# The order of the SBUF pools in a two-layer hybrid trunk: weights low, activations in the middle

## The chip, the core and the metric

The kernel runs as one program on one core of one Trainium2 chip. The core has a matrix engine (TensorE, PE in the rows; its weight loads are rows of PEld), a vector engine (DVE), a scalar engine (ACT), a helper engine (POOL, GpSimd) and a queue engine (SP) that issues the transfers between HBM and the on-chip memory SBUF. SBUF has 128 partitions; a tile takes the same byte range in each of them, so that one byte address per tile says where it lies. Matrix results go to a second memory, PSUM. The metric is the device time of one execution in microseconds (us); the kernel before takes 2235.08 us, median of 3 runs (2234.99 to 2235.28).

## The reference

One sequence of 1024 tokens with 1024 channels goes through two layers. All weights and activations are float32.

```python
# layer 0: h = rms_norm(x);  x += lru_sb_mixer(h)
proj = h @ w_in                                     # 1024 -> 512 gate, 512 rec, 3 x 512 q,k,v
y_lru = gelu(gate) * rg_lru(conv4(x_rec), ...)      # linear recurrence over time
y_sb  = stick_breaking_attention(q, k, v)           # 8 heads of 64, blocks of 128 queries
x = x + concat(y_lru, y_sb) @ w_out
# layer 1: h = rms_norm(x);  x += conformer_conv_module(h)
u = h @ pw1_w + pw1_b
u = u[:, :1024] * sigmoid(u[:, 1024:])
u = causal_depthwise_conv(u, dw_w) + dw_b           # width 31
x = x + silu(layer_norm(u)) @ pw2_w + pw2_b
# after each layer: h = rms_norm(x);  a = relu(h @ w1);  x += (a * a) @ w2   (1024 -> 4096 -> 1024)
# at the end: rms_norm(x) * final_g
```

## The kernel before, in words

The sequence is worked on in two chunks of 512 tokens (a and b in the names of the rows, `_a` and `_b`). Every large product is made from three matmuls: each float32 operand is split into a high part and a low part in the type float32r (`wh`, `wl` for weights; `hh`, `hl`, `ah`, `al`, `y..h`, `y..l`, `s..h`, `s..l` for activations), and `mm3` (lines 153 to 160) adds low-high, high-low and high-high into one PSUM bank. Each of these matmuls has a stationary operand of 128x128, read by a weight load (PEld) of 128 columns, that is 512 bytes of each partition, and a moving operand of 128x512, that is 2048 bytes of each partition. There are two forms:

- `colmm` (lines 161 to 163): a weight slice is stationary and a normed activation moves. It makes `xg`, `q`, `k` (input projection), `pg`, `pv` (the Conformer's first projection, `pw1`), and `m` (first half of the MLP, `m1` inside `mlp`). Per output tile: 8 slices of the contraction, 3 matmuls each, 24 in all.
- `rows_into_x` (lines 235 to 240) and `v_cols`: an activation slice is stationary and a weight row moves. It makes `v`, `o_wo` (output projection), `o_q` (the Conformer's second projection, `pw2`), and `o_a`, `o_b` (second half of the MLP, `m2`). Per output tile of the last three: 4 slices, 12 matmuls.

In 512-column float32r matmuls that is 3072 of `m`, 3072 of `o_a` and `o_b`, 768 of `pg` and `pv`, 384 each of `xg`, `o_q` and `o_wo`, 192 each of `q`, `k` and `v`, and 96 of the attention's `z`.

Where the tiles lie is decided by pools. A pool takes a contiguous range of SBUF when it is opened, each range above the one before, in the order of the `tc.tile_pool` lines; inside a pool each tag has its slots (`bufs`) one after the other. The pools are:

- `cp` (line 43): constants, among them the identity of the transposes. A 64-byte tile `pad_cp` is part of it.
- `hp_` (line 44, 48 slots of 2048 bytes): the residual `x` and every split activation that is not the MLP's: `hh`, `hl`, `y..h`, `y..l`, `s..h`, `s..l`, also the attention's `ks` and `vt`. `ht`, `hf` and `xt_` (lines 52 to 59) take from it.
- `wp` (line 45): two raw weight buffers of 8192 bytes, which the transfers fill, and four each of `wh` and `wl` of 4096 bytes, which ACT and DVE write (`split_w`, `col_units`) and TensorE reads.
- `lp` (line 46, 8 slots): the convolution's inputs `u` and the recurrent branch's tiles, taken by `lt`.
- `sp` (line 47): small statistics; a 64-byte tile `pad_sp` (line 50) is its first.
- above them, by turns in the same range, `p1` (attention and recurrence: tags a, q, r and the gate weights `gaw`, `gxw`) and `p2` (tag b, 11 slots for the MLP's `r`, `ah`, `al`; tag c, 9 slots).

The order of the instructions on each engine comes from a scheduler that works from dependencies and modelled durations, together with hand-written pacing (`paced`, `waiting`, `tc.issue_after`, `tc.high_priority`).

Of the kernel before, what the change touches and what calls it, by code (L numbers as in the profile page):

```python
# [31 lines left out]
def tile_hybrid_trunk(  # L32
# [8 lines left out]
    V, A, T, Q = nc.vector, nc.scalar, nc.tensor, nc.gpsimd  # L41

    cp = ctx.enter_context(tc.tile_pool(name="cp", bufs=1))
    hp_ = ctx.enter_context(tc.tile_pool(name="hp", bufs=48))
    wp = ctx.enter_context(tc.tile_pool(name="wp", bufs=4))
    lp = ctx.enter_context(tc.tile_pool(name="lp", bufs=8))
    sp = ctx.enter_context(tc.tile_pool(name="sp", bufs=12))
    ps = ctx.enter_context(tc.tile_pool(name="ps", bufs=2, space=PSUM))

    sp.tile([P, 16], F32, tag="pad", bufs=1, name="pad_sp")  # L50
# [742 lines left out]
```

## Time and profile before

| What | Value |
|---|---|
| median of 3 runs | 2235.08 us |
| the profiled execution: its own time | 2235.9 us |
| its span, first to last instruction | 2234.1 us |
| TensorE busy | 2195.6 us (98%), 10180 matmuls |
| DVE, ACT, POOL busy | 1412.5, 954.3, 110.6 us (63%, 43%, 5%) |
| chain that ended last: PE, DVE, ACT | 95%, 3%, 1% |
| mean granted TensorE clock | 0.996 |

A matmul's row has its start and a recorded length. Matmuls overlap in the pipeline, so that the recorded length (389 ns in undisturbed stretches) is longer than the distance from one start to the next; this distance is what a stretch costs, and it is a stretch's length over its number of matmuls. The recorded length follows it: when the next start comes 6 ns later, it is some 6 ns longer.

### The profile page before, as it was taken

Reading aid. Unit: us, or ns where it says so; the run is one execution under the profiler, and the core shown is the slowest. Engines: PE = TensorE matmul, PEld = TensorE weight load, DVE = VectorE, ACT = ScalarE, POOL = GpSimd, SP = SyncE. Lnnn points to the kernel's source line nnn. Section 1 sums busy time; section 2 is a strip of 40 time slices with the busy share of each in tenths; the row PEclk is TensorE's granted clock in tenths of the full one; section 3 lists DMA queues with packets and bytes.
Section 4 is the critical chain, followed back from the end, with each engine's and each line's share of the span. In section 5 each row is a group of like instructions: output and inputs, shape, how many; then the busy total and the mean of one; then the engine's idle time right before and its main releaser. Section 6 shows DMA issues by size and latency. Waiting matters only on the chain.

```text
span 2234.1 us, 25970 instructions
## 1 busy us (share of the span) xinstructions
PE 2195.6 (98%) x10180; PEld 1770.6 (79%) x10180; DVE 1412.5 (63%) x1934; ACT 954.3 (43%) x1509; POOL 110.6 (5%) x296
## 2 busy tenths in 40 slices
PE   7999999999999999999999999999999999999998
PEld 5877776688888888888888888788888888888887
DVE  4387877855443444479898664999886555444344
ACT  4467677535333334333333363433333535333332
POOL 1000000000000001100000010300000001000000
PEclk9999999999999999999999999999999999999999
DMA  4111014012222223332223223233232234222222
GB/s 159 57 41 36 34 53 151 27 59 76 95 94 94 95 95 99 108 100 82 93 96 108 81 94 94 85 97 99 89 99 91 93 106 140 95 95 95 95 94 76
DMA packets 172010, 199.25 MB, mean 89 GB/s; under 512 B 5648, under 2 KB 120688, under 8 KB 171888
## 3 DMA queue, kind: packets, MB, share of 16 engines
q1 hardware_dynamic: 171872, 197.59, 27.2%
q8 instruction: 80, 1.31, 0.2%
q14 instruction: 42, 0.34, 0.0%
q10 hardware_dynamic: 16, 0.00, 0.0%
HBM read 190.23 MB, written 7.34 MB: 88 GB/s over the span
## 4 chain that ended last, share of the span: by engine, by line
PE 95%; DVE 3%; ACT 1%; issue 1%; DMA 0%; POOL 0%; SPq 0%; DVEq 0%; POOLq 0%; ACTq 0%
PE o_b L157 5%; PE o_a L157 5%; PE o_b L158 5%; PE o_a L159 5%; PE o_b L159 5%; PE o_a L158 5%; PE m_a L157 5%; PE m_a L159 5%; PE m_b L159 5%; PE m_b L157 5%; PE m_a L158 5%; PE m_b L158 5%; PE av L529 2%; PE wt L521 1%; PE xg L158 1%; PE xg L157 1%
## 5 line engine op out<-in xcount | busy, mean ns | idle before, releaser
L647 DVE SCALAR_TENSOR_TENSOR cv<-u,dwT,cv 128x512 f32<-128x512 f32 x480 | 340.0, 754 | 0.2
L157 PE MATMUL o_a<-wh_w2a,al_a 128*128 128x512 f32 x512 | 202.4, 396 | 0.0
L157 PE MATMUL o_b<-wh_w2b,al_b 128*128 128x512 f32 x512 | 202.3, 395 | 0.0
L158 PE MATMUL o_a<-wl_w2a,ah_a 128*128 128x512 f32 x512 | 202.2, 395 | 0.0
L159 PE MATMUL o_b<-wh_w2b,ah_b 128*128 128x512 f32 x512 | 202.1, 395 | 0.0
L158 PE MATMUL o_b<-wl_w2b,ah_b 128*128 128x512 f32 x512 | 202.1, 395 | 0.0
L159 PE MATMUL o_a<-wh_w2a,ah_a 128*128 128x512 f32 x512 | 201.6, 395 | 0.0
L125 ACT CAST wh_w1b<-raw_w1b 128x1024 fp32r<-128x1024 f32 x64 | 67.2, 1050 | 219.4 <-PE o_b L159 200.9
L125 ACT CAST wh_w1a<-raw_w1a 128x1024 fp32r<-128x1024 f32 x64 | 67.1, 1051 | 213.3 <-PE o_a L159 203.6
L105 DVE TENSOR_TENSOR wl_w2a<-raw_w2a,wh_w2a 128x1024 fp32r<-128x1024 f32 x64 | 78.3, 1223 | 124.1 <-ACT wh_w2a L104 124.1
L105 DVE TENSOR_TENSOR wl_w2b<-raw_w2b,wh_w2b 128x1024 fp32r<-128x1024 f32 x64 | 80.3, 1254 | 118.2 <-ACT wh_w2b L104 118.2
L240 DVE TENSOR_TENSOR xr<-o_a,xr 128x512 f32<-128x512 f32 x128 | 87.5, 686 | 81.0 <-PE o_a L159 80.1
L240 DVE TENSOR_TENSOR xr<-o_b,xr 128x512 f32<-128x512 f32 x128 | 87.9, 687 | 76.5 <-PE o_b L159 75.5
L159 PEld LDWEIGHTS o_b<-wh_w2b,ah_b 128*128 128x128 f32 x512 | 96.5, 188 | 22.5
L159 PEld LDWEIGHTS o_a<-wh_w2a,ah_a 128*128 128x128 f32 x512 | 96.5, 188 | 22.4
L158 PEld LDWEIGHTS o_b<-wl_w2b,ah_b 128*128 128x128 f32 x512 | 96.5, 188 | 22.3
L158 PEld LDWEIGHTS o_a<-wl_w2a,ah_a 128*128 128x128 f32 x512 | 96.5, 188 | 22.1
L157 PEld LDWEIGHTS o_a<-wh_w2a,al_a 128*128 128x128 f32 x512 | 96.4, 188 | 22.2
L157 PEld LDWEIGHTS o_b<-wh_w2b,al_b 128*128 128x128 f32 x512 | 96.4, 188 | 22.2
L252 ACT ACTIVATE r_b<-m_b 128x512 f32<-128x512 f32 x64 | 38.4, 600 | 169.3 <-PE m_b L159 169.3
L252 ACT ACTIVATE r_a<-m_a 128x512 f32<-128x512 f32 x64 | 38.4, 600 | 164.1 <-PE m_a L159 159.7
L126 DVE TENSOR_TENSOR wl_w1b<-raw_w1b,wh_w1b 128x1024 fp32r<-128x1024 f32 x64 | 77.9, 1220 | 37.9 <-ACT wh_w1b L125 37.9
(537 smaller groups left out, 5344.4 us busy)
## 6 DMA issues: line engine op xcount, KB each, us to landing
raw_w1a<-in_mlp_w_dram SPq DMA_DIRECT2D x32, 1024.0 KB, 5.1
raw_w2a<-in_mlp_w_dram SPq DMA_DIRECT2D x32, 1024.0 KB, 5.1
raw_w1b<-in_mlp_w_dram SPq DMA_DIRECT2D x32, 1024.0 KB, 5.2
raw_w2b<-in_mlp_w_dram SPq DMA_DIRECT2D x32, 1024.0 KB, 5.0
raw_pw<-in_od_pw_w_dram SPq DMA_DIRECT2D x32, 512.0 KB, 4.5
raw_q<-in_od_pw_w_dram SPq DMA_DIRECT2D x8, 1024.0 KB, 4.9
raw_wo<-in_ev_w_out_dram SPq DMA_DIRECT2D x6, 768.0 KB, 5.2
xa<-in_x_dram SPq DMA_DIRECT2D x16, 256.0 KB, 5.2
```

Source lines behind the costliest of these rows:

```text
L105: paced(V.tensor_tensor(lo, raw, hi.bitcast(F32), op=ALU.subtract), 1)
L125: A.copy(hi, srcs[i])
L126: paced(V.tensor_tensor(lo, srcs[i], hi.bitcast(F32), op=ALU.subtract), 2)
L157: T.matmul(acc, ll, rh, start=(i == 0), stop=False)
L158: T.matmul(acc, lh, rl, start=False, stop=False)
L159: T.matmul(acc, lh, rh, start=False, stop=(i == n - 1))
L240: paced(V.tensor_tensor(xt[t][h], acc, xt[t][h], op=ALU.add), 1.5)
L252: A.activation(r, acc, AF.Relu)
L521: T.transpose(pt[:, b * P:(b + 1) * P], ke[:, b * P:(b + 1) * P], ident)
L529: ins = T.matmul(av[j * 64:j * 64 + 64, tt * P:(tt + 1) * P], vt[lo_s // P + b][:, hc:hc + 64], wts[j][:, b * P:(b + 1) * P], start=(diag ...
L647: waiting.append(lambda k=k, m=m: V.scalar_tensor_tensor(cv[m], u[m][:, k:k + C], dwT[:, k * KT + m:k * KT + m + 1], cv[m], op0=ALU.mult, ...
```

## The change

The line that opens `hp_` moves from second to fifth place. Nothing else in the program is changed; the line numbers after it go up by one.

```diff
     cp = ctx.enter_context(tc.tile_pool(name="cp", bufs=1))
-    hp_ = ctx.enter_context(tc.tile_pool(name="hp", bufs=48))
+
     wp = ctx.enter_context(tc.tile_pool(name="wp", bufs=4))
     lp = ctx.enter_context(tc.tile_pool(name="lp", bufs=8))
     sp = ctx.enter_context(tc.tile_pool(name="sp", bufs=12))
+    hp_ = ctx.enter_context(tc.tile_pool(name="hp", bufs=48))
     ps = ctx.enter_context(tc.tile_pool(name="ps", bufs=2, space=PSUM))
```

The instructions of all five engines stand in the same order as before, with the same tiles in the same slots of their pools and the same semaphore waits. What differs is the byte address of every tile of four pools. In bytes of a partition:

| Pool | Before | After | First byte modulo 256, before and after |
|---|---|---|---|
| `wp`: raw, then `wh`, `wl` | 118528 to 167680 | 20224 to 69376 | 0 and 0 |
| `lp` | 167680 to 185088 | 69376 to 86784 | 0 and 0 |
| `sp` | 185088 to 187776 | 86784 to 89472 | 0 and 0 |
| `hp_` | 20224 to 118528 | 89472 to 187776 | 0 and 128 |
| `p1`, `p2` | from 187776 | from 187776 | 128 and 128 |

The slots of `hp_` (2048 bytes), of `wh` and `wl` (4096) and of `p2` (2048) are multiples of 256, and each stationary slice is 512 bytes, so that every such operand has its pool's remainder modulo 256. Exceptions above 187776 are the attention's `q` tiles in `p1` (212736 and up) and `gaw`, `gxw` (200448, 202496), all at remainder 0 because of the sizes of the slots below them; and the slots of `lp`, 2176 bytes apart, are at 0 and 128 by turns.

## Rows read from the trace of the kernel before

**Rows 1.** The page: engines with their busy time, then the chain by engine

```profile
PE 2195.6 (98%) x10180; PEld 1770.6 (79%) x10180; DVE 1412.5 (63%) x1934; ACT 954.3 (43%) x1509; POOL 110.6 (5%) x296
...
PE 95%; DVE 3%; ACT 1%; issue 1%; DMA 0%; POOL 0%; SPq 0%; DVEq 0%; POOLq 0%; ACTq 0%
```

**Rows 2.** Whole kernel by stage: start:end length, PE busy (instructions), clock, DMA share, GB/s

```profile
0.00:110.00 110.00, 95.11 (x431) 1.00 0.34 109
110.00:510.00 400.00, 387.51 (x2130) 0.98 0.18 58
510.00:2232.00 1722.00, 1712.95 (x7623) 1.00 0.29 95
```

**Rows 3.** Four stretches: `m`, `pg` and `pv`, `o_b`, `o_q`; PE, columns as above

```profile
576.33:592.65 16.32, 16.32 (x73) 1.00 0.19 70
932.84:1019.87 87.03, 87.03 (x385) 1.00 0.33 99
1036.20:1058.51 22.31, 22.31 (x97) 1.00 0.30 94
1815.11:1836.86 21.75, 21.75 (x97) 1.00 0.29 97
```

**Rows 4.** Groups of matmuls, whole kernel: line, tiles, count, busy us, mean ns

```profile
L159 PE MATMUL o_b<-wh_w2b,ah_b 128*128 128x512 f32 x512 | 202.1, 395 | 0.0
...
L159 PE MATMUL m_a<-hh_ma,wh_w1a 128*128 128x512 f32 x256 | 100.0, 390 | 0.0
...
L159 PE MATMUL xg<-hh_e,wh_xg 128*128 128x512 f32 x128 | 51.8, 405 | 0.0
...
L157 PE MATMUL v<-wh_v,hl_e 128*128 128x512 f32 x64 | 27.6, 436 | 0.0
...
L157 PE MATMUL pg<-hh_ob,wl_pw 128*128 128x512 f32 x64 | 25.1, 392 | 0.0
...
L157 PE MATMUL o_wo<-wh_wo,y00l 128*128 128x512 f32 x8 | 3.8, 471 | 1.3 <-DVE xr L240 0.9 <-DVE y00l L168 0.4
```

**Rows 5.** Matmuls from `m` to `o_b`, in order of time: start us, recorded us

```profile
1035.74 0.39 PE L158 MATMUL m_b<-hl_m,wh_w1b 128*128 128x512 f32 x1
1035.97 0.40 PE L159 MATMUL m_b<-hh_m,wh_w1b 128*128 128x512 f32 x1
1036.20 0.40 PE L157 MATMUL o_b<-wh_w2b,al_b 128*128 128x512 f32 x1
```

**Rows 6.** The `o_b` stretch of Rows 3 and the matmul before it, by group

```profile
L157 PE MATMUL o_b<-wh_w2b,al_b 128*128 128x512 f32 x32 | 12.6, 395 | 0.0
...
L159 PE MATMUL m_b<-hh_m,wh_w1b 128*128 128x512 f32 x1 | 0.4, 396 | 0.0
```

**Rows 7.** One `o_a` matmul among `m_a`, 534.4 to 535.1 us, by group

```profile
L159 PE MATMUL m_a<-hh_m,wh_w1a 128*128 128x512 f32 x2 | 0.8, 392 | 0.0
L157 PE MATMUL o_a<-wh_w2a,al_a 128*128 128x512 f32 x1 | 0.4, 397 | 0.0
L157 PE MATMUL m_a<-hh_m,wl_w1a 128*128 128x512 f32 x1 | 0.4, 389 | 0.0
```

**Rows 8.** `z` between `q` matmuls, 240.1 to 240.9 us, by group

```profile
L158 PE MATMUL q<-hl_e,wh_qk 128*128 128x512 f32 x1 | 0.4, 389 | 0.0
L498 PE MATMUL z<-ks,q 128*128 128x512 f32 x1 | 0.4, 389 | 0.0
L499 PE MATMUL z<-ks,q 128*128 128x512 f32 x1 | 0.4, 389 | 0.0
```

**Rows 9.** `pr` (plain float32) with its moving tile at 167680, 102.4 us, by group

```profile
L407 PE MATMUL pr<-xc,gaw 128*128 128x512 f32 x2 | 1.0, 590 | 0.0
```

**Rows 10.** `pr` with its moving tile at 169856, 377.3 us, by group

```profile
L407 PE MATMUL pr<-xc,gaw 128*128 128x512 f32 x2 | 1.0, 592 | 0.0
```

**Rows 11.** The longest waits of PE: for whom, us in total, times, longest

```profile
PE nps_e L214 <- DVE hl_e L220: 6.5, 2, 4.9
...
PE z L498 <- DVE ks L564: 3.6, 1, 3.6
```

## The prediction

> **What bounds the kernel now.** I read first the page's engine lines and the chain of waits [rows 1]: TensorE is busy for 98% of the span and holds 95% of the chain; DVE has 3%, ACT 1%, transfers none. The stretches [rows 2] say where that holds: from 510 us on TensorE is busy for 1712.95 of 1722.00 us, and the matmuls simply follow each other; before, in attention and start, it idles 14.9 and 12.5 us. So the time is the number of matmuls times the distance from one start to the next, and the question is whether an address can change that distance.
>
> For this I took four undisturbed stretches at the full granted clock of 1.00 (the 2.4 GHz level) and divided the length by the number of matmuls that the code gives [rows 3] (the instruction counts there have one more, at the edge):
> - `m`, 3 tiles of 24: 16.32 us / 72 = 226.7 ns
> - `pg`, `pv`, 16 tiles of 24: 87.03 / 384 = 226.6 ns
> - `o_q`, 8 tiles of 12: 21.75 / 96 = 226.6 ns
> - `o_b`, 8 tiles of 12: 22.31 / 96 = 232.4 ns
>
> `o_q` and `o_b` come from the same lines, with the same shapes and types. What differs is where the stationary slice lies: `o_q` loads it from `hp_` (remainder 0 modulo 256), `o_b` from `p2` (remainder 128). The moving rows are `wp`'s in both, at remainder 0. The 5.8 ns are thus tied to the tile's place, and the whole kernel shows them too: o's groups record 395 ns, m's 390 [rows 4].
>
> What about the place does it? The step from `m` to `o_b` helps [rows 5, 6]: already the last `m` matmul, during which the first slice of `p2` is loaded, records 396 ns against 389, while it still streams its own moving tile from low in `hp_`. A single `o_a` matmul between `m` matmuls shows the same: the `m` matmul before it brings the mean of two to 392 (389 and 396), the `o_a` itself records 397, the next one is back at 389 [rows 7]; one such load costs some 15 ns (7 and 8) when it stands alone. It isn't height as such: `z` loads its stationary `q` slices from `p1`, at 212736 and above, but at remainder 0, and records 389 with its neighbours [rows 8]. So the sign is the odd multiple of 128, either of the load alone or of the load against the moving stream.
>
> **The change part by part.** No instruction is removed, added or moved, and no wait changes. What changes is the remainder of `hp_`: 0 before, 128 after; `wp`, `lp`, `sp`, `p1` and `p2` keep theirs. Three classes of full-rate matmuls follow.
>
> *Unchanged, 3072 `o_a`, `o_b`:* stationary from `p2` (128), moving from `wp` (0), as before. 0 us.
>
> *Stationary from `hp_`, moving from `wp`: 384 `o_q`, 384 `o_wo`, 192 `v`.* This becomes the pair of remainders that `o_b` has today, so its distance is shown by a row. `o_q`: 384 x 5.8 ns = 2.2 us. `o_wo` and `v` are already partly off the 226.6 ns beat (471 and 436 ns in their first groups [rows 4]), so I take half: 576 x 2.9 = 1.7 us. Together +3.9 us; the bounds are 0 and 960 x 5.8 = 5.6.
>
> *Moving from `hp_`, stationary from `wp`: 3072 `m`, 768 `pg` and `pv`, 384 `xg`, 384 `q` and `k`, 96 `z`, the last with its stationary slice in `p1`.* Now the moving tile has 128 and the load 0. No full-rate row has this pair. The nearest row is `o_b`, which is the same pair with the roles exchanged: the two operands differ by 128. If the two reads of one partition disturb each other, only their difference counts, and the price is again 5.8 ns. What supports a disturbance between the two reads rather than a slow load: the plain float32 matmuls `pr` record 590 and 592 ns, two instructions for one product, with a moving tile at remainder 0 and at 128 [rows 9, 10]; at that slower pace the remainder is worth nothing. The same rows are the bound from the other side: a moving tile at 128 costs 0 to 2 ns. I take `o_b`'s price, because it alone is a full-rate float32r row:
> - `m`: from the recorded means, 395 - 390 = 5 ns less rounding (the twelve groups average 390.1, the six of o 394.9): 3072 x 4.8 = 14.9 us
> - `pg`, `pv` (392 ns in the group shown, 390.4 over all twelve): 768 x 4.5 = 3.5 us
> - `xg`, `q`, `k`: already at 405 ns in the group shown, half of the price: 768 x 2.9 = 2.2 us
> - `z`: 96 x 5.8 = 0.6 at most; taken as 0
>
> Together +20.6 us; the bounds are 0 and 4704 x 5.8 = 27.3, if it is the same price, and more if the moving operand has its own (a rival below).
>
> *What I cost at nothing.* DVE, ACT and POOL read and write `hp_` too, and transfers fill `xa`, `xr` and `yr` there. DVE and ACT are busy for 63% and 43% of the span [rows 1], and PE's longest waits for them total 6.5 and 3.6 us [rows 11]; TensorE's stream covers them from 510 us on. If that cover were gone, DVE's 3% of the chain, some 67 us, would be what can stretch: 1% of it is 0.7 us.
>
> The sum: 2235.9 us of the profiled execution + 3.9 + 20.6 = 2260.4; the runs' median is 0.8 us below that execution, so 2259.6, and I say 2260.
>
> **The rivals.**
>
> *Only the load's own address counts.* Then `m`, `pg`, `xg`, `q`, `k` stay at 226.7 ns and only the 960 matmuls with a slice from `hp_` slow down: 2235.1 + 3.9 = 2239.0, between 2235 and 2240.7. For it: `pr`'s two rows, and that the penalty starts with the first load from `p2` [rows 6]. Against it: the loads are busy for 1770.6 us and the matmuls for 2195.6 [rows 1], so a slightly slower load has room to hide, yet the matmuls spread.
>
> *The moving operand pays a price of its own.* It is four times as long as a slice. With the single event's 15 ns on each of 4608 matmuls (`m`, `pg`, `pv`, `xg`, `q`, `k`): +69, and with the 3.9 a time of 2308; with four times 5.8 ns it would be +107. Nothing in the trace shows it, and `pr` speaks against it.
>
> *The other side: distance, not remainder.* `o` is the one class that has both operands above 134912; all others have one in `hp_`, at most at 118528. If neighbours in the upper part disturb each other, the change carries `wp` to the bottom and frees `o`: 3072 x 5.8 = 17.8 us less, 2217. It decides as soon as `o`'s distance falls by more than the 24.5 us / 3072 = 8 ns that the other terms cost, or by anything if these are 0. Against it: the last `m` matmul with its 396 ns [rows 6], whose moving tile lies below 118528; and the new middle place puts part of `hp_` beside `p2`.
>
> *Nothing happens:* the 5.8 ns belong to `p2` for another reason, and 2235 stays. For it: `o` is also the only class whose slices DVE and ACT have just written into `p2`; against it, `o_q`'s slices are just as fresh.
>
> The Trainium skill is on the side of this last rival: its page "SBUF — State Buffer", section "Who interferes with whom", gives TensorE two independent read ports, one for the moving operand and one for the weight load, and says that it never waits on anyone. By that no address could matter and the time would be 2235. The trace doesn't agree: 226.6 against 232.4 ns for the same instructions [rows 3].
>
> **How the numbers follow.** Likeliest case (difference of remainders): 0.48, its own range 2250 to 2268, the upper end with 5.8 ns on all 5664 matmuls concerned (+33). Load alone: 0.24. Own price of the moving operand: 0.07. Distance: 0.11. Nothing: 0.10. The range from 2234 to 2272 holds the first, the second and nearly all of the last; distance and own price are left out. A measurement of this kernel tells a difference from none at about 0.2%, 4.5 us, so that faster is below 2230.6 and slower above 2239.6. Slower: 0.48 + 0.07 + nearly half of the load-alone case, 0.11 = 0.66. Same: the other 0.13 + 0.10 = 0.23. Faster: 0.11.
>
> **What the changed profile would show.** In the stretches of [rows 3]: `o_b` at 232.4 ns as before; `o_q` at 232.4 instead of 226.6, which settles that the remainder of the load matters at all; `m` and `pg` at about 232 if the difference counts, at 226.7 if the load alone counts, above 235 if the moving tile pays for itself. The groups of `m` and `pg` would record about 395 instead of 390 and 392. The prediction is wrong if `m` stays at 226.7 (then the step in which I exchanged the roles fails), or if `o_b` falls below 230 (then it was distance).

## The result, and the profile after

The changed kernel takes 2267.97 us (median of 4 runs, 2267.02 to 2269.30), the kernel before 2235.03 us (4 runs, 2234.68 to 2235.28): a ratio of 1.0148, 95% interval [1.0130, 1.0165], or 32.9 us more. Predicted were 2260 us, in a range of 2234 to 2272, and slower with a chance of 0.66.

The page of the kernel after, the lines that answer to [rows 1]:

```profile
span 2265.2 us, 25970 instructions
...
PE 2227.0 (98%) x10180; PEld 1772.9 (78%) x10180; DVE 1415.3 (62%) x1934; ACT 954.3 (42%) x1509; POOL 109.9 (5%) x296
...
PE 94%; DVE 3%; ACT 1%; issue 1%; DMA 0%; POOL 0%; SPq 0%; DVEq 0%; POOLq 0%; ACTq 0%
```

TensorE is busy for 31.4 us more, with the same 10180 matmuls; the span is 31.1 us longer. DVE and ACT do the same work in nearly the same time (DVE 2.8 us more), and the shares of the chain are as they were, within a point. The stages of the kernel after (start:end length, PE busy (instructions), clock, DMA share, GB/s; they answer to [rows 2]):

```profile
0.00:110.00 110.00, 95.07 (x427) 1.00 0.34 109
110.00:515.00 405.00, 392.54 (x2136) 0.98 0.18 58
515.00:2263.00 1748.00, 1739.41 (x7620) 1.00 0.29 93
```

The clock is as before. The third stage, in which TensorE hardly waits, holds most of the loss: it is some 26 us longer, and busy for 26.5 us more. The longest waits of PE after (us in total, times, longest), against [rows 11]:

```profile
PE nps_e L215 <- DVE hl_e L221: 6.2, 2, 4.6
...
PE z L499 <- DVE ks L565: 3.4, 1, 3.4
```

Each is a little shorter, and all of PE's idle time, span less busy time, is 38.2 us against 38.5, so nothing of the loss is waiting. It lies in the distance between matmuls. The four stretches of [rows 3] in the kernel after, `m`, then `pg` and `pv`, `o_b`, `o_q` (columns as in the stages):

```profile
581.55:598.34 16.79, 16.79 (x73) 1.00 0.19 64
943.24:1032.83 89.59, 89.59 (x385) 1.00 0.31 96
1049.64:1072.03 22.39, 22.39 (x97) 1.00 0.30 94
1840.09:1862.48 22.39, 22.39 (x97) 1.00 0.28 94
```

Divided by 72, 384, 96 and 96 matmuls, all four run at 233.2 to 233.3 ns from one start to the next. (The windows are cut to 10 ns; the distances in the tables below come from the starts themselves and can differ from such a quotient by 0.2 ns.) Three of them ran at 226.6 or 226.7 before, `o_b` at 232.4. The groups over the whole kernel (count | busy us, mean ns), against [rows 4]; the line numbers are one higher:

```profile
L160 PE MATMUL o_b<-wh_w2b,ah_b 128*128 128x512 f32 x512 | 202.3, 395 | 0.0
...
L160 PE MATMUL m_a<-hh_ma,wh_w1a 128*128 128x512 f32 x256 | 101.2, 395 | 0.0
...
L160 PE MATMUL xg<-hh_e,wh_xg 128*128 128x512 f32 x128 | 52.6, 411 | 0.0
...
L158 PE MATMUL v<-wh_v,hl_e 128*128 128x512 f32 x64 | 27.6, 436 | 0.0
...
L158 PE MATMUL pg<-hh_ob,wl_pw 128*128 128x512 f32 x64 | 25.7, 401 | 0.0
...
L158 PE MATMUL o_wo<-wh_wo,y00l 128*128 128x512 f32 x8 | 3.5, 434 | 1.7 <-DVE xr L241 1.4 <-DVE y00l L169 0.4
```

`m` now records what `o` records, 395 ns. For the sum by class I took every distance from one matmul's start to the next in both traces and booked it to the class of the first of the two (us, waits included):

| Class | before | after | difference | predicted |
|---|---|---|---|---|
| `m` | 700.3 | 717.6 | +17.3 | +14.9 |
| `pg`, `pv` | 178.5 | 183.9 | +5.4 | +3.5 |
| `xg`, `q`, `k` | 188.3 | 191.2 | +2.9 | +2.2 |
| `o_q` | 87.6 | 89.8 | +2.2 | +2.2 |
| `o_wo`, `v` | 142.1 | 142.3 | +0.2 | +1.7 |
| `o_a`, `o_b` | 715.3 | 716.9 | +1.6 | 0 |
| all others (transposes, `av`, `z`, ...) | 211.7 | 213.1 | +1.3 | 0 |

Such a sum holds waits too: e1 and e2 below run `pg` and `pv` at the same distance and book 180.0 and 178.4 us for them. Differences of 1 to 2 us in this table are therefore weak.

### The profile page after: what moved, and what is told of

Its sections match the earlier page's. It is cut to its first block, busy times and chain, and to the rows that moved or that the text cites. A ratio compares the mean times of both kernels' runs of the same rounds, so it can differ in the third digit from the quotient of the medians.

```text
span 2265.2 us, 25970 instructions
## 1 busy us (share of the span) xinstructions
PE 2227.0 (98%) x10180; PEld 1772.9 (78%) x10180; DVE 1415.3 (62%) x1934; ACT 954.3 (42%) x1509; POOL 109.9 (5%) x296
## 4 chain that ended last, share of the span: by engine, by line
PE 94%; DVE 3%; ACT 1%; issue 1%; DMA 0%; POOL 0%; SPq 0%; DVEq 0%; POOLq 0%; ACTq 0%
PE m_a L158 5%; PE o_b L159 5%; PE m_b L160 5%; PE m_b L159 5%; PE o_b L160 5%; PE o_b L158 5%; PE m_b L158 5%; PE o_a L160 5%; PE o_a L159 5%; PE o_a L158 5%; PE m_a L159 5%; PE m_a L160 5%; PE av L530 2%; PE xg L159 1%; PE wt L522 1%; PE xg L160 1%
## 5 line engine op out<-in xcount | busy, mean ns | idle before, releaser
L159 PE MATMUL o_a<-wl_w2a,ah_a 128*128 128x512 f32 x512 | 202.3, 395 | 0.0
L159 PE MATMUL o_b<-wl_w2b,ah_b 128*128 128x512 f32 x512 | 202.3, 395 | 0.0
L159 PEld LDWEIGHTS o_b<-wl_w2b,ah_b 128*128 128x128 f32 x512 | 96.2, 188 | 23.0
L159 PEld LDWEIGHTS o_a<-wl_w2a,ah_a 128*128 128x128 f32 x512 | 96.3, 188 | 22.6
```

What stands on the lines that cost most here:

```text
L159: T.matmul(acc, lh, rl, start=False, stop=False)
```

## Experiments

The change moves two things at once: the order and distance of the pools, and the remainder of `hp_` modulo 256. Pads in the existing pools separate them. A small pad makes a pool longer by 128 bytes or less, and `bufs=8` on `nb` makes `sp` shorter by 128, so that the pools' remainders can be chosen in either order. In all nine kernels each engine's instructions stand in the order of the kernel before, and nothing of the computation is left out. In the classes of the table above, all others left out, every operand has its pool's remainder as given here. Below, "difference" is the remainder of the stationary slice that is loaded minus that of the moving tile, modulo 256.

| Run | order of the pools | remainders of `wp`, `hp_`, `p2` | median us | ratio to before, 95% | `m`, `pg`/`pv`, `o_b`, `o_q`, ns |
|---|---|---|---|---|---|
| before | old | 0, 0, 128 | 2235.03 | | 226.7, 226.6, 232.4, 226.6 |
| after | new | 0, 128, 128 | 2267.97 | 1.0148 [1.0130, 1.0165] | 233.3 in all |
| e1 | new | 0, 0, 0 | 2218.41 | 0.9917 [0.9900, 0.9933] | 226.7 in all |
| e2 | old | 0, 0, 0 | 2218.12 | 0.9916 [0.9901, 0.9931] | 226.7 in all |
| e3 | old | 128, 128, 128 | 2219.29 | 0.9923 [0.9908, 0.9937] | 226.7 in all |
| e4 | old | 0, 128, 128 | 2267.44 | 1.0137 [1.0122, 1.0152] | 233.3 in all |
| e5 | new | 0, 0, 128 | 2235.66 | 0.9997 [0.9987, 1.0007] | 226.7, 226.7, 232.4, 226.7 |
| d1 | new | 0, 64, 192 | 2238.65 | 1.0013 [1.0003, 1.0024] | 228.9, 228.9, 229.0, 233.3 |
| d2 | new | 0, 32, 96 | 2271.61 | 1.0159 [1.0138, 1.0181] | 233.3, 233.3, 234.2, 233.3 |
| d3 | new | 0, 96, 160 | 2268.94 | 1.0147 [1.0126, 1.0169] | 233.3, 233.3, 233.3, 234.3 |
| x1 | old | `wh` 0, `wl` 128; 0; 0 | 2247.33 | 1.0052 [1.0029, 1.0075] | 231.0, 231.1, 228.9, 233.4 |

The kernel before, run beside them, took 2237.15 us (e1 to e4), 2236.33 (e5, d1 and the other two d) and 2236.45 (x1).

### e1 and e2: all at remainder 0, in the new and in the old order

```diff
-    sp.tile([P, 16], F32, tag="pad", bufs=1, name="pad_sp")
+    sp.tile([P, 48], F32, tag="pad", bufs=1, name="pad_sp")
```

> The new order of the pools, with the 64-byte pad at the start of sp made 192 bytes, so that hp_, p1 and p2 rise by 128 bytes: wp, hp_ and p2 are then all at remainder 0 modulo 256 (the q tiles and gaw, gxw in p1 go to 128). Difference theory (only the difference of the two operands' remainders counts): every large class falls to 226.7 ns, o_a and o_b included, 3072 x 5.8 ns = 17.8 us below the kernel before: 2217 us. Order theory (the new places themselves cost): m stays near 232-233 ns and the time above 2250 us. If the period were 512 bytes rather than 256 (wp is at 256 modulo 512, hp_ and p2 at 0 here), all classes would be slow, 2266 us or more.

> The old order, with the same 128 bytes more of pad at the start of sp: only p1 and p2 move, by 128 bytes; wp, hp_ and p2 are all at remainder 0 modulo 256. Difference theory: m, pg, o_q stay at 226.7 ns, o_a and o_b fall from 232.4 to 226.7: 2235 - 17.8 = 2217 us, the same as with the new order. Theory that o is slow because both its operands lie high: o stays at 232.4 ns, 2235 us. Theory that p2 is slow for another reason (fresh slices): 2235 us.

The four stretches of e2, in the order used so far:

```profile
575.97:592.28 16.31, 16.31 (x73) 1.00 0.21 68
927.77:1014.80 87.03, 87.03 (x385) 1.00 0.32 100
1031.13:1052.88 21.75, 21.75 (x97) 1.00 0.31 96
1802.11:1823.86 21.75, 21.75 (x97) 1.00 0.30 97
```

`o_b` falls from 22.31 us [rows 3] to 21.75 us for its 96, 226.6 ns, the beat of the others. Over the 3072 matmuls of `o_a` and `o_b` that makes 3072 x 5.8 ns = 17.8 us; 18.7 and 19.0 were measured, as the difference theory had it; the order theory and a period of 512 bytes are refuted. The order makes no difference: 2218.41 against 2218.12. Both kernels beat the two of this case, by 0.8% and 2.2%, for 128 bytes of a pad. In e1 `wp` lies at 256 modulo 512 and the others at 0, in e2 also `hp_` at 256, with the same beat: 256 is enough as the period.

### e3: all at remainder 128, in the old order

```diff
-    cp.tile([P, 16], F32, name="pad_cp")
+    cp.tile([P, 48], F32, name="pad_cp")
...
-            nb = sp.tile([P, 1], F32, tag="nb", name=f"nb{c}{t}")
+            nb = sp.tile([P, 1], F32, tag="nb", bufs=8, name=f"nb{c}{t}")
```

> The old order, with cp's pad 128 bytes larger (wp, lp and hp_ rise by 128) and the nb tag of sp cut from 12 to the 8 slots it uses (p1 and p2 stay): wp, hp_ and p2 are all at remainder 128. Difference theory: all differences are 0, so m, o, pg, o_q run at 226.7 ns and the time is 2217 us, although no operand is at a multiple of 256. Theory of each operand's own remainder (128 costs, whoever has it): every class is at 232.4 ns or, with both operands at 128, up to 238 ns: 2266 to 2300 us. Theory that only the load's remainder counts is excluded by m in the changed kernel already; it would give m at 232.4 here too.

The stretches of e3:

```profile
576.19:592.50 16.31, 16.31 (x73) 1.00 0.21 69
928.00:1015.03 87.03, 87.03 (x385) 1.00 0.35 100
1031.36:1053.11 21.75, 21.75 (x97) 1.00 0.30 96
1804.06:1825.81 21.75, 21.75 (x97) 1.00 0.29 97
```

In the large classes every load and every moving tile has the remainder that looked like the culprit before, and all four stretches run at 226.7 ns. So no operand pays for its own address: "load alone" and "own price" fall together, and the difference stands.

### e4: the remainders of the changed kernel in the old order

```diff
-    cp.tile([P, 16], F32, name="pad_cp")
+    cp.tile([P, 48], F32, name="pad_cp")
...
+    gp = ctx.enter_context(tc.tile_pool(name="gp", bufs=1))
+    gp.tile([P, 32], F32, name="pad_gp")
```

(`gp` is opened behind `hp_`; `nb` gets `bufs=8` and the two `st` tags `bufs=10`, so that `p2` comes to 128.)

> The old order with the remainders of the changed kernel: cp's pad is 128 bytes larger, so hp_ is at 128; a pool of 128 bytes between hp_ and wp puts wp and lp back to 0; nb and st in sp are cut to the slots they use, so p1 and p2 keep their place at 128. Difference theory, and every theory of remainders: m, pg, o_q, o at 232.4 to 233.5 ns, 2266 to 2269 us as with the change. Order theory: the old places bring the old time, 2235 us.

`m` and `o_q` of e4:

```profile
582.63:599.42 16.79, 16.79 (x73) 1.00 0.20 64
...
1841.90:1864.29 22.39, 22.39 (x97) 1.00 0.28 94
```

233.2 ns in both, and 2267.44 us: the whole loss without the change of order.

### e5: the new order with the remainders of before

```diff
+    gp = ctx.enter_context(tc.tile_pool(name="gp", bufs=1))
+    gp.tile([P, 32], F32, name="pad_gp")
...
-            nb = sp.tile([P, 1], F32, tag="nb", name=f"nb{c}{t}")
+            nb = sp.tile([P, 1], F32, tag="nb", bufs=8, name=f"nb{c}{t}")
```

> The new order with the remainders of the kernel before: nb cut to 8 slots, so that hp_ starts at remainder 0, and a pool of 128 bytes above hp_, so that p1 and p2 keep their place at 128. Difference theory: m, pg, o_q at 226.7 ns, o at 232.4: the old time, 2235 us (2237 on this chip if the last call's values of before hold). Order theory: some of the 33 us stay.

`m` and `o_b` of e5:

```profile
578.50:594.82 16.32, 16.32 (x73) 1.00 0.21 68
...
1038.37:1060.68 22.31, 22.31 (x97) 1.00 0.31 94
```

These are the lengths of [rows 3], and the time is that of before (0.9997, [0.9987, 1.0007]). With e4 this settles the question of the order: the pools' order and distances are worth nothing, within 0.1%.

### d1, d2, d3: other differences than 0 and 128

The edits are those of e5 with other sizes: `pad_sp` of 32, 24 and 40 elements instead of 16, `pad_gp` of 32, 16 and 16.

> How the distance depends on the difference. The new order; nb is cut to 8 slots and the pad in sp set so that hp_ starts at remainder 64, and a small pool above hp_ puts p1 and p2 at 192; wp stays at 0. Load minus moving operand, modulo 256: o_q, o_wo, v +64; o_a, o_b +192; m, pg, pv, xg 192 (0 minus 64). If any difference that isn't a multiple of 256 costs the same: all at 232 to 233 ns, about 2267 us. If only the odd 128 costs (two halves of 128 bytes, and 64 still in the same half): smaller, about half, 229 to 230 ns for 64 and 192. If there is a difference at which the reads never meet: below 226.7 ns.

> The same with hp_ at remainder 32 and p1, p2 at 96: o_q, o_wo, v +32; o_a, o_b +96; m, pg, pv, xg 224. Any difference costs the same: all at 232 to 233 ns, about 2267 us. Cost in proportion to the distance from a multiple of 256: o_q and m at 228 to 229 ns (a quarter of 5.8), o at 231 ns (three quarters), about 2250 us.

> The same with hp_ at remainder 96 and p1, p2 at 160: o_q, o_wo, v +96; o_a, o_b +160; m, pg, pv, xg 160. Any difference costs the same: all at 232 to 233 ns, about 2267 us. In proportion: all at 231 ns (three quarters of 5.8), about 2260 us.

All four stretches of d1:

```profile
578.83:595.30 16.47, 16.47 (x73) 1.00 0.20 67
934.17:1022.06 87.89, 87.89 (x385) 1.00 0.32 98
1038.55:1060.52 21.97, 21.97 (x97) 1.00 0.30 95
1817.30:1839.70 22.40, 22.40 (x98) 1.00 0.27 94
```

`pg`/`pv` and `o_b` of d2:

```profile
945.65:1035.24 89.59, 89.59 (x385) 1.00 0.31 96
1052.05:1074.52 22.47, 22.47 (x97) 1.00 0.31 93
```

`pg`/`pv` and `o_q` of d3:

```profile
942.86:1032.45 89.59, 89.59 (x385) 1.00 0.31 96
...
1840.37:1862.85 22.48, 22.48 (x97) 1.00 0.27 94
```

These stretches sorted by difference, all runs but x1 together:

| Difference | distance, ns | seen in |
|---|---|---|
| 0 | 226.6 to 226.7 | before, e1, e2, e3, e5 |
| 32 | 233.3 | d2 `o_q` |
| 64 | 233.3 | d1 `o_q` |
| 96 | 234.2, 234.3 | d2 `o_b`, d3 `o_q` |
| 128 | 232.4 to 233.3 | before, after, e4, e5 |
| 160 | 233.3 | d3 `m`, `pg`/`pv`, `o_b` |
| 192 | 228.9 to 229.0 | d1 `m`, `pg`/`pv`, `o_b` |
| 224 | 233.3 | d2 `m`, `pg`/`pv` |

In these stretches two classes with different operands and different remainders of their own agree wherever their difference is the same (96, 160, 192). Of the expectations, "any difference costs the same" holds within 1.3 ns for all but 192 (d2 and d3 come to 2271.61 and 2268.94 us); a price in proportion to the distance from a multiple of 256 is refuted by 32, which costs as much as 64; "about half" holds for 192 and fails for 64.

But 192 has no one price. In d1 the first `xg` matmuls, whose difference is 192 as well, run at 22.39 us / 96 = 233.2 ns, directly behind `v`. Later 24 `xg` matmuls, behind a pause and nine matmuls at the lower clock level, run at 5.49 / 24 = 228.8:

```profile
69.54:91.93 22.39, 22.39 (x97) 1.00 0.32 94
129.09:134.58 5.49, 5.49 (x25) 1.00 0.00 0
```

These are the same class, the same difference and the same granted clock (1.00), at two distances. So a difference other than 0 brings a price, but it doesn't fix by itself how high the price is, and that 64 costs 6.6 ns and 192 mostly 2.3 can't be put down to the sign alone.

### x1: only the low parts of the weights at 128

```diff
-    waiting, credit = [], [0.0]
+    waiting, credit, padded = [], [0.0], []
...
+        if not padded:
+            padded.append(wp.tile([P, 32], F32, tag="padw", bufs=1, name="pad_wl"))
```

(with `pad_sp` of 48 elements and `bufs=8` on `nb`; the pad stands ahead of the first `wl`.)

> One operand of three. The old order with everything at remainder 0 as in e2_old_order_all0, except that a pad of 128 bytes in wp puts the four wl buffers (the low parts of the weights) at 128; nb is cut to 8 slots, so p1 and p2 don't move further. In colmm one load of three (wl) now differs from its moving tile by 128, in rows_into_x one moving tile of three. If the price is per pair of reads, in proportion: 226.9 + 5.8 / 3 = 228.8 ns for m and for o, 2218 + 8640 x 1.9 ns = 2235 us. If each pair that stands alone costs what the single o_a matmul among m matmuls cost, about 13.6 ns: 231.4 ns, 2257 us. If only loads or only moving tiles mattered, m alone or o alone would slow down.

Here one matmul of three has its weight at 128, every other operand of the large classes is at 0. The `pg`/`pv`, `o_b` and `o_q` stretches of x1:

```profile
938.75:1027.49 88.74, 88.74 (x385) 1.00 0.32 97
1044.13:1066.10 21.97, 21.97 (x97) 1.00 0.30 95
1828.21:1850.61 22.40, 22.40 (x97) 1.00 0.28 94
```

The `pg` groups within the first of them, where the weight is what is loaded (`pv`'s are alike):

```profile
L159 PE MATMUL pg<-hh_oa,wl_pw 128*128 128x512 f32 x64 | 25.4, 397 | 0.0
...
L161 PE MATMUL pg<-hh_oa,wh_pw 128*128 128x512 f32 x64 | 25.3, 396 | 0.0
...
L160 PE MATMUL pg<-hl_oa,wh_pw 128*128 128x512 f32 x64 | 24.9, 389 | 0.0
```

The `o_b` groups within the second, where the weight moves:

```profile
L160 PE MATMUL o_b<-wl_w2b,ah_b 128*128 128x512 f32 x32 | 12.6, 395 | 0.0
L159 PE MATMUL o_b<-wh_w2b,al_b 128*128 128x512 f32 x32 | 12.4, 389 | 0.0
L161 PE MATMUL o_b<-wh_w2b,ah_b 128*128 128x512 f32 x32 | 12.4, 388 | 0.0
```

In program order L161 comes just ahead of the next L159. The trace has each load start some 3 ns after the matmul before its own. So a lone load at 128 delays two matmuls, the one during whose stream it is read (396) and the one that uses it (397), as in [rows 7]; a lone moving tile at 128 delays only itself (395). The stretches say the same: (231.1 - 226.7) x 3 = 13.2 ns for each such load, (228.9 - 226.7) x 3 = 6.6 ns for each such moving tile, against 6.6 ns for each matmul where all are off. `m` comes out as by the expectation's second reading (231.4 ns), `o_b` as by its first (228.8), so that neither held as a whole, and 2247.33 us lies between their 2235 and 2257. That both slowed refutes "only loads" and "only moving tiles".

`o_q` at 233.4 ns has the same pairs of remainders as `o_b`. Its slices lie at 256 modulo 512 where `o_b`'s lie at 0, but that isn't needed to explain it: the same trace has 42 `o_a` matmuls in a row, just behind transposes, at `o_q`'s distance, 9.80 us / 42 = 233.3 ns, while the long `o_a` stretches behind `m` run at 228.9:

```profile
1517.22:1527.02 9.80, 9.80 (x43) 1.00 0.35 107
```

Start to start, `o_q` and these `o_a` matmuls repeat 230, 236, 234 ns; the stretches behind `m` repeat 234, 226, 227. The same class with the same remainders can thus run in two rhythms. What makes a rhythm stays open.

## Why the prediction was right, and where its sizes were off

**That TensorE's beat sets the time** held: all but 1.3 us of the longer time from start to start is in the classes that the prediction names, and the waits got no longer.

**That a stationary slice at 128 against a moving tile at 0 costs `o_b`'s price** held for `o_q`: 2.2 us predicted, 2.2 measured. I had half the price for `o_wo` and `v`, 1.7 us; they cost 0.2. The first group of `v`, in the start stage, records 436 ns in both kernels: off the beat, the addresses are worth next to nothing.

**That the roles can be exchanged** was the step on which most of the sum rested, with no row of before behind it. The `m` stretch at 233.3 ns is what it asked for, and e3, e4 and e5 show its reason: with both operands at 128 nothing is lost, with one of them at 128 the loss is there in either order.

**The size** was short by 6.6 us (24.5 against the 31.1 of the span), mostly in three terms. (3072 x 4.8 ns is 14.7 us and not 14.9, a slip of 0.2.) `m` was priced at 4.8 ns from recorded means, which over the whole kernel differ by no more than that; start to start it is 6.6 ns in the undisturbed stretch and 17.3 us / 3072 = 5.6 ns over all: 2.4 us. `pg` and `pv` were priced the same way, at 4.5 ns, and paid 5.4 us / 768 = 7.0, waits included, against 6.7 in the stretch: 1.9 us. And `o`, called unchanged, went from 232.4 to 233.3 ns: 1.6 us. That the result, 32.9 us, meets the upper end of the likeliest case, 5.8 ns on all 5664 matmuls (+33), is luck: `m` paid less than that over all, `o_wo` and `v` next to nothing, and `o`, which isn't in that sum, made up for part of it.

Why is `o` slower after the change, at unchanged remainders? Its addresses don't tell: in e5 both its operands lie where they lie after the change, and it runs at 232.4 ns. The starts tell more. Before, `o_b` repeats eight distances from 228 to 241 ns, 232.4 in the mean; after, mostly 229 and 238 by turns, 233.3 in the mean. Both rhythms occur in the kernel after: the 24 `m_a` matmuls and the 96 of `o_a` behind them that follow here run in the first, at 232.1 and 232.3 ns, as do three more such `o_a` stretches up to 1716 us; the `o_b` stretch shown above, with the same pair of remainders, runs in the second.

```profile
1554.19:1559.76 5.57, 5.57 (x25) 1.00 0.46 175
1559.76:1582.06 22.30, 22.30 (x97) 1.00 0.30 95
```

So one pair of remainders has two rhythms, and a long stretch keeps its own to the end. The `m` matmuls ahead do not settle which: behind `m` in the second rhythm `o` always runs in the second, behind `m` in the first it is found in either. What decides stays open. The prediction priced every class by its own addresses alone and had no term for this.

**The rivals.** "Load alone" (2239) is refuted by `m` and by e3, "own price" (2308) by e3 and by `m`'s 233.3 ns. "Distance" (2217) is refuted by e4 and e5; its time did turn up in e1 and e2, but there it comes from the remainder, since both orders give it. "Nothing happens" (2235) is refuted by the result. The Trainium skill's page "SBUF — State Buffer", section "Who interferes with whom", calls TensorE's two read ports independent and says that it never waits on anyone; the measured 226.7 and 233.3 ns for the same instructions, with nothing but addresses between them, decide against that here. What in the reads collides, no run shows. The `pr` rows [rows 9, 10], one of the grounds of the prediction, were not tested further.

## What to carry to other kernels

Where TensorE's stream is the bound and each matmul brings its own weight load (shown here for float32r, loads of 128x128 and moving tiles of 128x512), place moving and stationary tiles at equal remainders modulo 256 bytes; 128 bytes of padding bought 0.8% here, and losing the match cost 1.5%. The order of the pools is worth nothing in itself, but any edit that moves a pool's start can change a remainder, so print the start addresses after each such edit. And price a change of the beat from stretch lengths divided by counts, not from recorded means.

## What was not expected of the hardware

- The price has no simple course: of the seven differences other than 0 that were run, six cost 5.8 to 7.6 ns, and 192 costs 2.2 to 2.3 ns for `m`, `pg`, `pv` and `o_b` and 6.6 in a stretch of `xg`. Smaller offsets (32, 64) cost as much as 128.
- One pair of remainders can run at two distances, each kept through a whole stretch: 232.3 and 233.3 ns in the kernel after, 228.8 and 233.2 in d1, 228.9 and 233.3 in x1. At the difference 0 every stretch shown ran at 226.6 to 226.7 ns.
- None of the stretches shown ran below 226.6 ns at any choice of addresses.
- Two operands that both lie at 128 are as good as two at 0 (e3, 2219.29 us against 2218.12), so that the address of one operand by itself tells nothing.
